# One channel tile of a 31-tap convolution: from VectorE's adds to products with diagonal matrices on TensorE

## The chip, the core and the metric

The kernel runs on one core of a Trainium2 chip. The metric is device time in microseconds (us). TensorE (PE in the rows) makes matrix products and writes them to PSUM, an on-chip memory of eight banks of 128 partitions by 512 fp32 values. VectorE (DVE), ScalarE (ACT) and GpSimd (POOL) work element by element; SyncE (SP) only issues DMA transfers here. Each engine executes its own instructions in the order of the program and waits where an operand isn't ready.

## What is computed

Two transformer blocks in fp32 on x of 512 tokens by 1024 channels. The first has a SwiGLU, two kinds of attention, gates and a second SwiGLU. The second has a mixer and a mixture of 32 experts. The change lies in the mixer:

```python
def hybrid_mixer(h, w_in, b_in, conv_w, conv_b, conv_ln_g, conv_ln_b, ...):
    z = jnp.einsum("bsd,de->bse", h, w_in) + b_in
    conv_a, conv_gate, q, k, v, o, i_pre, f_pre = jnp.split(z, ...)
    u = conv_a * jax.nn.sigmoid(conv_gate)
    u = causal_depthwise_conv(u, conv_w, conv_b)          # 31 taps, 512 channels
    u = jax.nn.silu(layernorm(u, conv_ln_g, conv_ln_b))
    qk = jax.nn.silu(causal_depthwise_conv(jnp.concatenate([q, k], axis=-1), qk_conv_w, qk_conv_b))
    ...                                                    # mlstm_chunkwise, 4 heads: hm
    y = jnp.concatenate([u, hm], axis=-1)
    return jnp.einsum("bse,ed->bsd", y, w_out)
```

A tap of the depthwise convolution multiplies a channel's row by one weight, shifts it by s tokens, and adds it to the sum.

## The kernel before

Activations lie with channels on the 128 partitions and the 512 tokens along the row, so 512 channels are four tiles. fp32 products are made of three fast ones: weights and activations are split into a high part and a rest (`hi` by a ScalarE copy, `lo` by a subtraction on VectorE or GpSimd), and high·high, high·rest and rest·high are added in a bank (`mm3`). `dense` is one output tile: 24 products for 1024 input channels. Its result lies in one of three banks with the tag `mm`, and VectorE must have read it before the bank is used again. Two banks have the tag `sc`, two `tp`, and one `po`.

`second_mixer` issues its work in this order:

- For each tile j of 0 to 3, two `dense` calls (the gate `cg` and `ca`). ScalarE makes the sigmoid, VectorE multiplies, and u_in[j] (named `ca` in rows) is ready.
- The recurrence gates: 24 products of the eight columns `wif`, read by VectorE as `zif`.
- `proj_rows`: 96 products for v into three `mm` banks and `po`. The gates' own chain (`recurrence`, tiles `ls_`, `ca_rows`, `cm_rows`, `em`) is issued between them, one step per point.
- Eight `dense` calls for q and k, each followed on VectorE by a 4-tap convolution (`late`, tiles `zq` and `qk`), and the four heads of the recurrence (`weights`, `head`; tiles `md`, `w`, `den`, `hm`).
- Four `dense` calls for the output gate `so`. Before the second, `conv_norm` issues what is left of the 31-tap convolution and starts its layer norm (`csum`, `csq`).
- The products with w_out, then the mixture of experts.

The 31-tap convolution writes `co[0]` to `co[3]` (`conv` in rows). VectorE makes tiles 0 and 1 and 19 taps of tile 2; ScalarE (multiply, `ctmp`) and GpSimd (add) make tile 3 and 12 taps of tile 2. GpSimd also makes the rests `wlo` of the weights. Where a tap stands is decided while the program is written: `fill` is called after and within the `dense` calls, and issues taps as long as VectorE's estimated work stays behind TensorE's by FILL[0]. The engines execute what this gives; nothing is decided on the chip.

Of the kernel before, what the change touches and what calls it, by code (L numbers as in the profile page):

```python
# [8 lines left out]
F32 = mybir.dt.float32  # L9
F32R = mybir.dt.float32r  # L10
I32 = mybir.dt.int32
BF16 = mybir.dt.bfloat16
AF = mybir.ActivationFunctionType
ALU = mybir.AluOpType
# [4 lines left out]
T = 512  # L19
# [49 lines left out]
    ("mlstm_norm_g_2", 4), ("subln_g", 1), ("conv_w", 124), ("qk_conv_w", 32),  # L69
]  # L70
VOFF = {}
_o = 0
# [62 lines left out]
def expert_stream(g, u, d):  # L135

    g = g.reshape(NE, 2, 4, 128, DE).transpose(0, 1, 3, 2, 4).reshape(NE, 2, 128, 2048)
    u = u.reshape(NE, 2, 4, 128, DE).transpose(0, 1, 3, 2, 4).reshape(NE, 2, 128, 2048)
    d = d.reshape(NE, 2, 2, 128, D).transpose(0, 1, 3, 2, 4).reshape(NE, 2, 128, 2048)
    return np.ascontiguousarray(np.stack([g[:, 0], u[:, 0], g[:, 1], u[:, 1], d[:, 0], d[:, 1]], axis=1))  # L140
# [13 lines left out]
def constants():  # L154
    c = np.zeros((128, 128 * 4 + 512 + 242), np.float32)
    i = np.arange(128)
    c[:, 0:128] = np.eye(128)
    c[:, 128:256] = 1.0
    c[:, 256:384] = i[:, None] < i[None, :]
    c[:, 384:512] = np.where(i[:, None] <= i[None, :], 0.0, BIG)  # L160
    c[:, 512:1024] = np.arange(512)[None, :]
    r = c[:, 1024:]
    r[:, 0] = i
    r[:, 1] = 128 * i
    r[:, 2:74] = np.arange(72)[None, :]
    r[:, 74:106] = NE - np.arange(NE)[None, :]
    r[:, 106:110] = 128 * np.arange(4)[None, :] + i[:, None] - 1024
    r[:, 110:114] = 128 * np.arange(4)[None, :]
    r[:, 114:242] = (i % 64)[None, :]
    rel = np.arange(640) - 511  # L170
    b = t5_bucket_of(rel)
    hot = np.zeros((32, 640), np.float32)
    hot[b, np.arange(640)] = 1.0
    sel = np.zeros((8, 512), np.float32)
    for h in range(4):
        sel[4 + h, h * 128:(h + 1) * 128] = 1.0
    return c, hot, sel


def lay_out(a):  # L180

    r = {}
    r["xT"] = np.ascontiguousarray(a["x"][0].reshape(4, 128, KC, 128).transpose(3, 0, 2, 1))
    r["wd"] = dense_stream(a)
    r["we"] = expert_stream(a["expert_w_gate_2"][0], a["expert_w_up_2"][0], a["expert_w_down_2"][0])
    v = dict(a)
    v["b_in"] = a["b_in_2"][0, :3072]
    v["conv_w"] = a["conv_w_2"][0]
    v["qk_conv_w"] = a["qk_conv_w_2"][0]
    cols = [np.ascontiguousarray(v[n]).reshape(-1, 128).T for n, k in VECS]  # L190
    r["vecs"] = np.ascontiguousarray(np.concatenate(cols, axis=1))
    r["rows"] = np.ascontiguousarray(np.concatenate([
        a["b_in_2"][0, 2048:2560], a["norm_ffn_g_2"][0], a["final_norm_g_2"],
        a["router_group_b_2"][0], a["router_expert_b_2"][0],
        a["lambda_q1"][0], a["lambda_k1"][0], a["lambda_q2"][0], a["lambda_k2"][0]])[None])
    r["w_if"] = np.ascontiguousarray(a["w_in_2"][0][:, 3072:3080].reshape(KC, 128, 8).transpose(1, 0, 2))
    r["b_if"] = np.ascontiguousarray(a["b_in_2"][0, 3072:3080].reshape(8, 1))
    wr = np.concatenate([a["router_group_w_2"][0], a["router_expert_w_2"][0]], axis=1)
    r["w_r"] = np.ascontiguousarray(wr.reshape(KC, 128, 36).transpose(1, 0, 2))
    r["rel_a"] = a["rel_bias_a"][0]  # L200
    r["t5"] = np.ascontiguousarray(a["t5_bias"].T)
    r["c_main"], r["c_hot"], r["c_sel"] = constants()
    return r
# [5 lines left out]
class Stream:  # L209
# [35 lines left out]
    def next(self, n=1):  # L245
        u, j = divmod(self.pos, 8)
        if j == 0:
            self.split_to(u + HL - 1)
            self.hl.pop(u - 1, None)
        self.pos += n  # L250
        hi, lo = self.hl[u]
        s = slice(j * 128, (j + n) * 128)
        return hi[:, s], lo[:, s]
# [63 lines left out]
class Kern:  # L317
# [594 lines left out]
    def second_mixer(self):  # L912
        nc, I = self.nc, self.I
# [4 lines left out]
        u_in = []  # L918
        conv_ready = [-1]
# [12 lines left out]
        V = nc.vector  # L932
# [15 lines left out]
        sel = self.u("sel")  # L948
        nc.gpsimd.dma_start(sel[0:8, :], I["c_sel"][:, 0:512])

        def tile_taps(j):
            V.tensor_scalar(co[j], u_in[j], cw(j, 30), self.vec("conv_b_2", j), op0=ALU.mult, op1=ALU.add)
            yield 1
            for s in range(1, 31 - (POOL_TAPS if j == 2 else 0)):
                V.scalar_tensor_tensor(co[j][:, s:], u_in[j][:, :T - s], cw(j, 30 - s), co[j][:, s:],
                                       op0=ALU.mult, op1=ALU.add)
                yield 1

        def dve_taps():
            g = {j: tile_taps(j) for j in range(3)}  # L960
            while g:
                for j in list(g):
                    if conv_ready[0] >= j:
                        if next(g[j], 0):
                            yield 1
                        else:
                            del g[j]
                if g and min(g) > conv_ready[0]:
                    yield 0
                if conv_ready[0] < 0:  # L970
                    yield 0
        dtaps = dve_taps()

        co = [self.v("conv") for _ in range(4)]
# [22 lines left out]
        ptaps = pool_taps()  # L997
# [7 lines left out]

        def fill(spare=0.0):

            while V.work + FILL[0] + spare < nc.tensor.work:
                if next(dtaps, 0) == 0:
                    break  # L1010
            while nc.gpsimd.work + FILL[1] < nc.tensor.work:
                if next(ptaps, 0) == 0:
                    break
            V.work = max(V.work, nc.tensor.work)
            nc.gpsimd.work = max(nc.gpsimd.work, nc.tensor.work - FILL[2])
# [15 lines left out]
        def point():  # L1031
            stages.point()
            fill()
# [12 lines left out]
        for j in range(4):  # L1046
# [6 lines left out]
            g, a = self.u("cg"), self.v("ca")  # L1053
# [8 lines left out]

        ps = self.mm()
        for c in range(KC):
            self.mm3(ps[0:8], (whl[0][:, c], whl[1][:, c]), n[c], c == 0, c == KC - 1)
        fill()
# [63 lines left out]
        v = self.proj_rows(rr, bias=bv, hook=point)  # L1132
# [75 lines left out]

        def conv_norm():

            for g in (dtaps, ptaps):
                for _ in g:
                    pass
            if POOL_TAPS:
                V.tensor_add(co[2], co[2], co2)
            stages.start(layer_norm())
# [40 lines left out]
        for i in range(8):  # L1257
            h, which = divmod(i, 2)
            j = 4 * which + h
            point()  # L1260
            ps = self.dense(n, half)
# [19 lines left out]
        for j in range(4):  # L1281
# [6 lines left out]
            ps = self.dense(n, half)  # L1288
            late = None
            o = self.u("so")  # L1290
# [5 lines left out]
        for m in range(KC):  # L1296
# [4 lines left out]
            ps = self.dense(y)  # L1301
# [3 lines left out]
        for m in range(KC):  # L1305
            ps = self.dense(hm, self.mixed_sums if m == KC - 1 else None)
            for f in range(2 if m == KC - 1 else 1):
                a = slice(2 * f, 2 * f + 2) if m == KC - 1 else slice(0, 4)
# [626 lines left out]
```

## Time and profile before

| | |
|---|---|
| median of 3 runs | 2005.67 us (2005.52 to 2008.32) |
| the profiled execution: its time | 2004.82 us |
| its span | 2003.0 us |
| TensorE busy | 1894.3 us, 95% |
| VectorE busy | 1087.9 us, 54% |
| ScalarE, GpSimd busy | 636.4 us, 381.8 us |
| mean granted TensorE clock | 0.978 of full speed |

The span runs from the first to the last instruction; 1.8 us of the execution lie outside it. Times within the span are counted from its start. A matmul's busy time includes its way through the array, and it overlaps the next, so TensorE can be called busy while it isn't at its peak rate. The mixer lies at 1113 to 1430 us, the experts behind it.

### The profile page before, as it was taken

The page shows a single profiled execution, that of the slowest core. Times are in us where ns is not written, and L with a number is a line of the kernel's source. Part 1 is how long each engine was busy: PE and PEld are TensorE (multiplying, and loading weights), DVE is VectorE, ACT ScalarE, POOL GpSimd, SP SyncE. Part 2 cuts the span into 40 slices and gives each one's busy share as a digit, 9 for nine tenths or more (in the row PEclk, how much of TensorE's full clock was granted, in tenths as well). Part 3 has the DMA queues.
Part 4 walks back from the last instruction along what each step waited for, and adds up shares of the span by engine and source line. Part 5 has one row for each costly group of instructions (what it writes and reads, how often), then busy time and mean ns, then how long its engine had stood idle before and what let it go on. Part 6 is the DMA issues. An engine that isn't in the chain of part 4 may idle for free.

```text
span 2003.0 us, 22137 instructions
## 1 busy us (share of the span) xinstructions
PE 1894.3 (95%) x8372; PEld 1299.0 (65%) x8372; DVE 1087.9 (54%) x1655; ACT 636.4 (32%) x1006; POOL 381.8 (19%) x293
## 2 busy tenths in 40 slices
PE   7999999999999999999999988779799999999995
PEld 5888888887777788888888766657543333333331
DVE  6443344423668565443444599988544444444445
ACT  4322233325555443331223333433232111111112
POOL 2000000106654351000001456643210000000001
PEclk9999999999999999999999998889999999999997
DMA  5234222322222122222222211111799999999991
GB/s 178 85 129 153 92 97 93 126 85 93 81 68 75 64 93 97 101 89 106 86 104 101 97 63 43 42 42 54 288 355 420 419 397 391 380 397 378 384 359 43
DMA packets 52440, 337.85 MB, mean 169 GB/s; under 512 B 5868, under 2 KB 8724, under 8 KB 13804
## 3 DMA queue, kind: packets, MB, share of 16 engines
q1 hardware_dynamic: 48396, 324.04, 42.2%
q0 software_dynamic: 3072, 9.24, 1.5%
q10 hardware_dynamic: 864, 3.15, 0.4%
q8 instruction: 67, 1.10, 0.2%
q14 instruction: 41, 0.34, 0.0%
HBM read 332.18 MB, written 8.16 MB: 170 GB/s over the span
## 4 chain that ended last, share of the span: by engine, by line
PE 81%; DVE 14%; issue 2%; ACT 1%; DMA 1%; POOL 1%; SPq 0%; POOLq 0%; ACTq 0%; DVEq 0%
PE mm L302 65%; PE sc L302 8%; PE tp L302 4%; DVE conv L302 4%; PE po L302 3%; DVE qk L302 2%; DVE score L302 1%; DVE x L302 1%; DVE att_s L302 1%; DVE rs_t L302 1%; DVE rs_y L302 0%; DMA x<-in_xT_dram 0%; DVE hm L302 0%; DMA raw<-in_wd_dram 0%; DVE rs_r L302 0%
## 5 line engine op out<-in xcount | busy, mean ns | idle before, releaser
L302 PE MATMUL mm<-nhi,whi 128*128 128x512 f32 x1120 | 446.8, 399 | 13.3 <-ACT whi L356 9.4
L302 PE MATMUL mm<-nlo,whi 128*128 128x512 f32 x1120 | 439.1, 392 | 1.6 <-DVE nlo L302 1.6
L302 PE MATMUL mm<-nhi,wlo 128*128 128x512 f32 x1120 | 438.5, 392 | 0.7 <-DVE wlo L302 0.7
L356 ACT ACTIVATE whi<-raw 128x1024 fp32r<-128x1024 f32 x220 | 231.2, 1053 | 306.8 <-PE mm L302 119.0
L302 DVE TENSOR_TENSOR wlo<-raw,whi 128x1024 fp32r<-128x1024 f32 x155 | 198.1, 1279 | 208.9 <-ACT whi L356 208.9
L302 PE MATMUL mm<-eraw,xb 128*64 128x512 f32 (+1 forms) x992 | 272.9, 602 | 0.0
L302 PEld LDWEIGHTS mm<-nhi,whi 128*128 128x128 f32 x1120 | 211.8, 189 | 62.7 <-ACT whi L356 9.4
L302 PEld LDWEIGHTS mm<-nlo,whi 128*128 128x128 f32 x1120 | 211.6, 189 | 47.1 <-DVE nlo L302 4.5
L302 PEld LDWEIGHTS mm<-nhi,wlo 128*128 128x128 f32 x1120 | 211.4, 189 | 46.5 <-DVE wlo L302 1.7
L302 POOL TENSOR_TENSOR wlo<-raw,whi 128x1024 fp32r<-128x1024 f32 x65 | 163.5, 2520 | 150.9 <-ACT whi L356 125.1
L302 PEld LDWEIGHTS mm<-eraw,xb 128*64 128x64 f32 (+1 forms) x992 | 81.9, 145 | 130.3 <-issue 120.5
L302 PE MATMUL sc<-eraw,hT 128*64 128x512 f32 (+1 forms) x512 | 140.1, 602 | 0.0
L302 PE MATMUL mm<-hhi,whi 128*128 128x512 f32 x352 | 136.9, 389 | 0.0
L302 PE MATMUL mm<-hlo,whi 128*128 128x512 f32 x352 | 136.9, 389 | 0.0
L302 PE MATMUL mm<-hhi,wlo 128*128 128x512 f32 x352 | 136.9, 389 | 0.0
L302 POOL TENSOR_TENSOR acc<-sq,sq 128x512 f32<-128x512 f32 x6 | 8.7, 1456 | 579.6 <-ACT sq L455 579.6
L302 DVE TENSOR_TENSOR x<-x,po 128x512 f32<-128x512 f32 x62 | 42.6, 687 | 125.4 <-PE po L302 125.3
L302 POOL TENSOR_SCALAR rs_v<-fss 128x1 f32<-128x1 f32 x3 | 0.6, 191 | 515.0 <-ACT eraw L1882 514.8
L1699 ACT ACTIVATE xb<-xs 128x512 f32 (+1 forms) x31 | 21.9, 706 | 233.1 <-PE mm L302 233.0
L302 DVE TENSOR_TENSOR up<-mm,row 128x512 f32<-128x512 f32 x44 | 30.4, 691 | 110.8 <-PE mm L302 110.8
L302 DVE SCALAR_TENSOR_TENSOR conv<-ca,vecs,conv 128x502 f32<-128x502 f32 (+18 forms) x78 | 88.0, 1183 | 0.2
L302 DVE TENSOR_TENSOR y<-sc,y 64x512 fp32r<-64x512 f32 (+1 forms) x64 | 44.1, 689 | 80.7 <-ACT y L1774 62.3
(448 smaller groups left out, 2641.7 us busy)
## 6 DMA issues: line engine op xcount, KB each, us to landing
eraw<-in_we_dram SPq DMA_DIRECT2D x192, 1024.0 KB, 8.0
raw<-in_wd_dram SPq DMA_DIRECT2D x109, 1024.0 KB, 4.8
bias_rows<-bias_by_distance SPq DMA_DIRECT2D x4, 960.0 KB
bias<-bias_rows POOLq DMA_DIRECT2D x12, 256.0 KB, 3.1
x_rows<-x ACTq DMA_DIRECT2D x4, 512.0 KB, 3.5
x<-in_xT_dram SPq DMA_DIRECT2D x3, 512.0 KB, 8.3
raw<-in_wd_dram SPq DMA_DIRECT2D x2, 512.0 KB, 8.9
out_dram<-eraw SPq DMA_DIRECT2D x2, 512.0 KB
```

The source lines that it names most:

```text
L302: return f(*a, **k)
L356: self.nc.scalar.activation(hi, raw, AF.Copy)
L1699: self.nc.scalar.activation(x[:, :, 0:m], self.xs[:, :, ds(row, m)], AF.Copy)
```

## The change

Tile 0 of the convolution leaves VectorE. A new generator, `pe_taps`, advances by one step at every `fill`. It splits tile 0's weights and u_in[0] into high part and rest. For each four taps ScalarE then makes eight diagonal matrices of 128x128 (identity times a weight column, `cdh` and `cdl`), and TensorE adds three products a tap into one bank of the `sc` ring, shifted by the tap. A shift must be even, so an odd tap starts one column later, and one VectorE operation on 15 columns adds what is left out. The weight table gets 31 more columns (`conv_r`). The gates' product takes the other `sc` bank in place of an `mm` bank.

```diff
+        def pe_taps():
+            while conv_ready[0] < 0:
+                yield 0
+            o = VOFF["conv_r"]
+            w = self.vecs[:, o:o + 31]
+            wd = self.u("cwd", F32R)
+            wd = wd[:, 0:31], wd[:, 31:62]
+            self.split_act(w, *wd)
+            uh, ul = self.u("cuh", F32R), self.u("cul", F32R)
+            self.split_act(u_in[0], uh, ul)
+            p = self.sc()
+            yield 1
+            for s0 in range(0, 31, 4):
+                m = range(s0, min(s0 + 4, 31))
+                d = self.u("cdh", F32R), self.u("cdl", F32R)
+                for t, a in zip(d, wd):
+                    for i, s in enumerate(m):
+                        nc.scalar.activation(t[:, i * 128:(i + 1) * 128], self.ident, AF.Copy,
+                                             scale=a[:, s:s + 1].bitcast(F32))
+                yield 1
+                for i, s in enumerate(m):
+                    dh, dl = (t[:, i * 128:(i + 1) * 128] for t in d)
+                    for a, b in ((dh, uh), (dh, ul), (dl, uh)):
+                        nc.tensor.matmul(p[:, s + s % 2:], a, b[:, s % 2:T - s], start=(s == 0 and a is dh and b is uh),
+                                         stop=(s == 30 and a is dl))
+                yield 1
+            nc.scalar.activation(co[0], p, AF.Identity, bias=self.vec("conv_b_2", 0))
+            V.scalar_tensor_tensor(co[0][:, 1:30:2], w[:, 1:30:2], u_in[0][:, 0:1], co[0][:, 1:30:2],
+                                   op0=ALU.mult, op1=ALU.add)
...
-            g = {j: tile_taps(j) for j in range(3)}
+            g = {j: tile_taps(j) for j in (1, 2)}
...
         def fill(spare=0.0):
+            next(petaps, 0)
...
-        ps = self.mm()
+        ps = self.sc()
         for c in range(KC):
             self.mm3(ps[0:8], (whl[0][:, c], whl[1][:, c]), n[c], c == 0, c == KC - 1)
...
-            for g in (dtaps, ptaps):
+            for g in (petaps, dtaps, ptaps):
```

The taps that stay on VectorE move forward. Before, in its instructions behind `zif` (the gates' product, just ahead of v), taps of the tiles conv_8100 (0), conv_8101 (1) and conv_8102 (2) stand between the steps of the recurrence, and go on up to `conv_norm`:

```order
L302 TENSOR_TENSOR zif_8500<-mm_8454,RR_8231 8x512
L302 COPY zt_8531<-tp_8526 128x32
L302 SCALAR_TENSOR_TENSOR conv_8101<-ca_8294,vecs,conv_8101 128x501
L302 SCALAR_TENSOR_TENSOR conv_8102<-ca_8371,vecs,conv_8102 128x506
L302 TENSOR_SCALAR ls_s_8534<-ls_e_8533 128x16
```

In the changed program, in the same place, the last tap of all stands ahead of `zif`, and behind it comes nothing of the convolution but the 15 columns:

```order
L303 SCALAR_TENSOR_TENSOR conv_8102<-ca_8460,vecs,conv_8102 128x495
L303 SCALAR_TENSOR_TENSOR conv_8102<-ca_8460,vecs,conv_8102 128x494
L303 TENSOR_TENSOR zif_8686<-sc_8621,RR_8231 8x512
L303 COPY zt_8717<-tp_8712 128x32
L303 TENSOR_SCALAR ls_s_8720<-ls_e_8719 128x16
```

So 50 operations for tiles 1 and 2 stand ahead of `zif` in place of 32 for tiles 0 to 2, none ahead of u_in[1], and the q and k stretch has none.

On ScalarE the diagonals stand between the sigmoids (`cg`) and the weights' high parts (`whi`); `ctmp` are the first products of GpSimd's taps. This is the changed program around the fourth tile's sigmoid (`cg_8605`), where before there was nothing between it and `conv`:

```order
L357 ACTIVATE whi_8543<-raw_8395 128x1024
L970 ACTIVATE cdh_8559<-cmain,cwd_8258 128x128 x4
L970 ACTIVATE cdl_8560<-cmain,cwd_8258 128x128 x4
L1090 ACTIVATE cg_8605<-cg_8605,vecs 128x512
L970 ACTIVATE cdh_8611<-cmain,cwd_8258 128x128 x4
L970 ACTIVATE cdl_8612<-cmain,cwd_8258 128x128 x4
L1016 ACTIVATE conv_8103<-ca_8606,vecs 128x512
L1019 ACTIVATE ctmp_8665<-ca_8606,vecs 128x511
```

The group that `cdh_8611` feeds stands behind a sigmoid that waits for VectorE.

On TensorE that group stands between the gates' product (`sc_8621`) and the first product of v (`mm_8692`), which followed each other before:

```order
L303 MATMUL sc_8621<-nhi_8063,wif_1352_8079 8x512
L303 MATMUL sc_8621<-nlo_8064,wif_1352_8079 8x512
L303 MATMUL sc_8621<-nhi_8063,wif_1353_8080 8x512
L303 MATMUL sc_8265<-cuh_8261,cdh_8611 128x488
L303 MATMUL sc_8265<-cul_8262,cdh_8611 128x488
L303 MATMUL sc_8265<-cuh_8261,cdl_8612 128x488
...
L303 MATMUL mm_8692<-whi_8397,nhi_7719 128x512
```

Six groups of 12 products stand ahead of the gates' product, this one behind it, and the last (9 products) behind the second of the eight steps of v. It waits for diagonals that ScalarE makes behind `zif` and the first two `ls_e`.

## Rows read from the trace of the kernel before

**Rows 1.** The page: VectorE's and TensorE's busy tenths in 40 slices (50 us each), granted clock.

```profile
PE   7999999999999999999999988779799999999995
DVE  6443344423668565443444599988544444444445
PEclk9999999999999999999999998889999999999997
```

**Rows 2.** The chain that ended last, by line, of 1147 to 1229 and 1229 to 1344.

```profile
by line: DVE conv L302 45.8%; PE mm L302 23.1%; issue 9.9%; PE po L302 7.1%; PE tp L302 4.9%; DVE ca L302 3.7%; ACT cg L1055 3.6%; DVE cg L302 2.3%; DVE zif L302 0.7%; DVE em L302 0.0%
by line: DVE qk L302 38.4%; DVE conv L302 32.9%; issue 5.1%; DVE csum L302 4.5%; ACT zq L1274 4.5%; DVE zq L302 4.2%; DVE w L302 4.2%; DVE vr L302 2.3%; DVE md L302 2.0%; DVE den L302 1.1%; ACT so L1292 0.6%; DVE hm L302 0.6%; DVE so L302 0
```

**Rows 3.** Windows: stretch, length, busy us (instructions) of each engine, granted clock, DMA.

```profile
core 0: us, PE busy (x) PEld busy (x) DVE busy (x) ACT busy (x) POOL busy (x), PEclk, DMA share, GB/s
1147.00:1192.00 45.00, 38.99 (x168) 29.27 (x166) 41.57 (x45) 14.32 (x18) 17.24 (x8) 0.96 0.14 47
1192.00:1229.00 37.00, 28.43 (x108) 22.01 (x108) 30.87 (x47) 14.96 (x22) 26.56 (x15) 0.79 0.16 58
1229.00:1344.00 115.00, 88.96 (x400) 68.74 (x400) 106.76 (x120) 44.21 (x82) 70.62 (x43) 0.88 0.13 46
```

**Rows 4.** Waits of TensorE at 1185 to 1344: in total, times, longest.

```profile
PE tp L302 <- DVE den L302: 18.3, 3, 9.1
PE tp L302 <- issue: 6.0, 1, 6.0
PE mm L302 <- DVE zif L302: 5.5, 1, 5.5
PE mm L302 <- DVE vr L302: 3.9, 1, 3.9
```

**Rows 5.** Windows of the tile conv alone (VectorE's, ScalarE's, GpSimd's part of the convolution).

```profile
1158.00:1184.00 26.00, 23.02 (x23) 0.00 (x0) 0.00 (x0) 1.00 0.24 81
1192.00:1224.00 32.00, 13.56 (x19) 0.00 (x0) 14.59 (x10) 0.76 0.19 67
1224.00:1239.00 15.00, 12.12 (x7) 0.00 (x0) 8.26 (x6) 0.89 0.19 70
```

**Rows 6.** Timeline of VectorE and GpSimd at 1158 to 1230: start, us, operation.

```profile
1158.00 0.75 DVE L302 SCALAR_TENSOR_TENSOR ca<-ca,vecs,cg 128x512 f32<-128x512 f32 x1 [0.20 <-ACT cg L1055]
1158.79 0.55 DVE L302 TENSOR_SCALAR conv<-ca,vecs 128x512 f32<-128x512 f32 x1
1191.60 0.67 DVE L302 TENSOR_TENSOR zif<-mm,RR 8x512 f32<-8x512 f32 x1
1208.66 2.68 DVE L302 SCALAR_TENSOR_TENSOR conv<-ca,vecs,conv 128x497 f32<-128x497 f32 x4
1218.40 6.49 POOL L302 TENSOR_TENSOR conv<-conv,ctmp 128x501 f32<-128x501 f32 x2
1220.48 3.29 DVE L302 SCALAR_TENSOR_TENSOR conv<-ca,vecs,conv 128x502 f32<-128x502 f32 x5
1223.93 5.89 DVE L302 SCALAR_TENSOR_TENSOR conv<-ca,vecs,conv 128x495 f32<-128x495 f32 x3
1224.85 2.81 POOL L302 TENSOR_TENSOR wlo<-raw,whi 128x1024 fp32r<-128x1024 f32 x1
```

**Rows 7.** The chain in order of time: an undisturbed run of products.

```profile
695.05 76.18 PE mm L302 x336
```

**Rows 8.** Timeline of ScalarE: three 128x128 operations in a row.

```profile
1247.68 0.39 ACT L1151 ACTIVATE w<-md,ca 128x128 f32<-128x128 f32 x1
1247.98 0.39 ACT L1153 ACTIVATE w<-mb,ca 128x128 f32<-128x128 f32 x1
1248.27 0.39 ACT L1151 ACTIVATE w<-md,ca 128x128 f32<-128x128 f32 x1
```

**Rows 9.** Timeline of TensorE: the end of `wif`, starts of v, of q, and of the norm.

```profile
1183.97 0.39 PE L302 MATMUL mm<-nhi,wif 128*8 128x512 f32 x1
1192.33 0.79 PE L302 MATMUL mm<-whi,nhi 128*128 128x512 f32 x1 [5.53 <-DVE zif L302]
1230.63 0.47 PE L302 MATMUL mm<-nhi,whi 128*128 128x512 f32 x1 [3.86 <-DVE vr L302]
1344.30 2.07 PE L302 MATMUL tp<-csum,cmain 128*128 128x512 f32 x2 [2.85 <-DVE csum L302]
```

**Rows 10.** Groups of VectorE at 1229 to 1344: busy, mean ns.

```profile
L302 DVE SCALAR_TENSOR_TENSOR conv<-ca,vecs,conv 128x491 f32<-128x491 f32 (+17 forms) x29 | 38.3, 1364 | 0.1
L302 DVE SCALAR_TENSOR_TENSOR qk<-zq,vecs,qk 128x511 f32<-128x511 f32 (+2 forms) x24 | 30.2, 1258 | 0.8
```

**Rows 11.** Groups of GpSimd at 1186 to 1344.

```profile
L302 POOL TENSOR_TENSOR conv<-conv,ctmp 128x492 f32<-128x492 f32 (+29 forms) x41 | 60.3, 1470 | 30.7 <-ACT ctmp L985 26.5 <-ACT ctmp L994 2.0
L302 POOL TENSOR_TENSOR wlo<-raw,whi 128x1024 fp32r<-128x1024 f32 x14 | 36.3, 2596 | 15.3 <-ACT whi L356 15.3
L302 POOL TENSOR_TENSOR hm<-hm,row 128x512 f32<-128x512 f32 x3 | 5.0, 1675 | 18.0 <-ACT row L430 18.0
```

**Rows 12.** Windows behind the mixer: the experts' stretch, columns as in the third group.

```profile
1450.00:1600.00 150.00, 146.44 (x628) 57.85 (x630) 72.33 (x138) 35.78 (x76) 7.53 (x9) 0.98 0.98 396
1600.00:1750.00 150.00, 150.00 (x560) 55.59 (x556) 69.05 (x110) 27.06 (x45) 0.00 (x0) 1.00 0.98 391
```

More of the change, by code (lines that the diff above doesn't have):

```diff
@@ L68 @@
     ("conv_b_2", 4), ("conv_ln_g_2", 4), ("conv_ln_b_2", 4), ("qk_conv_b_2", 8),
-    ("mlstm_norm_g_2", 4), ("subln_g", 1), ("conv_w", 124), ("qk_conv_w", 32),
+    ("mlstm_norm_g_2", 4), ("subln_g", 1), ("conv_w", 124), ("qk_conv_w", 32), ("conv_r", 31),
 ]
@@ L189, in lay_out @@
     v["qk_conv_w"] = a["qk_conv_w_2"][0]
+    v["conv_r"] = a["conv_w_2"][0][::-1, 0:128]
     cols = [np.ascontiguousarray(v[n]).reshape(-1, 128).T for n, k in VECS]
@@ L949, in second_mixer @@
         nc.gpsimd.dma_start(sel[0:8, :], I["c_sel"][:, 0:512])
+        def pe_taps():
[27 more added lines that the diff above has]
+                                   op0=ALU.mult, op1=ALU.add)
+        petaps = pe_taps()
         def tile_taps(j):
```

## Prediction

> **What bounds the kernel now.** The first view is the page's table of slices [rows 1]. TensorE is at 9 tenths nearly everywhere, except in a dip in slices 24 to 29 (8 8 7 7 9 7), where VectorE is at its fullest (9 9 9 8 8 from slice 24). There lies the second mixer. The second view, the chain of work that ended last, read for the mixer alone [rows 2], shows why: at 1147 to 1229 us VectorE's taps (`conv`) hold 45.8% of it, TensorE's `mm` 23.1%; at 1229 to 1344 VectorE's `qk` holds 38.4%, its taps 32.9%, and TensorE is hardly there. The third, the windows [rows 3], gives the room: at 1229 to 1344 VectorE is busy 106.76 us of 115, TensorE 88.96, at a granted clock of 0.88; at 1192 to 1229 TensorE is busy 28.43 of 37. The fourth, TensorE's waits [rows 4], names VectorE each time: for `den` 18.3 us, `zif` 5.5, `vr` 3.9, and 6.0 put down to nothing while the recurrence's small VectorE steps run between taps. So in this stage, and only here, a tap on VectorE is on the path, and work on TensorE partly isn't.
>
> Ahead of 1184 it is the other way. TensorE runs the first dense products and `wif` without a gap, the last of them at 1183.97 [rows 9], while VectorE lags behind. Work put in there is paid in full.
>
> **What the change removes.** 31 operations (one on tensor and scalar, 30 two-tensor adds) leave VectorE. Two prices stand in the rows. In the mean a tap took 1.36 us at 1229 to 1344 [rows 10] and 1.00 at 1158 to 1184 (23.02 by 23) [rows 5]. But four taps in a row took 2.68, or 0.67 each, while GpSimd was idle [rows 6]. What lies between is GpSimd: five taps took 3.29 while two GpSimd adds took 6.49, against 1.47 for one in the mean [rows 6, 11]; and three taps took 5.89 around a `wlo` of 2.81 [rows 6]. One side stands while the other runs. If a tap's blocked time goes away with it, 31 taps at (1.00+1.36)/2 = 1.18 give 36.6 us. If the blocked time goes to the next operation, they give 31 x 0.67 = 20.8.
>
> The Trainium skill, "SBUF — State Buffer", section "Who interferes with whom", says that VectorE and GpSimd share one pair of ports as an exclusive lock: a VectorE instruction with two SBUF inputs and a GpSimd instruction that reads SBUF wait for each other, for the whole instruction. By that rule GpSimd's hold on the port stays and a tap gives back its own 0.67, so the stage could gain 20.8 us at most; by the mean price 36.6. The trace agrees with it in both directions in the rows just read. I take the sum below, which counts stretch by stretch, and keep 36.6 for the low end.
>
> **What it adds.** TensorE: 93 products of 496.5 columns in the mean (512 less the even shifts 0 to 30). 336 products of 512 columns took 76.18 us, 0.227 each [rows 7], so 0.22 each and 20.5 us in all. ScalarE: 62 diagonals. Operations of this size start 0.30 us apart [rows 8], so 18.6 us, two thirds of them ahead of 1192, where ScalarE is busy 14.32 of 45 [rows 3]: room enough, except where a group stands behind something late (below). VectorE: two subtractions and the 15 columns, together below 1.5 us, the first two while it would wait for u_in[1]: nothing. The wider weight table is 31 columns more in a load of 269: nothing. The bank of the `sc` ring is read by ScalarE during v, before a head asks for it: nothing; without that cover head 0 would wait for the rest of v.
>
> **The stage, stretch by stretch.**
>
> First, up to v. VectorE has nothing to do for tile 0 now and starts its taps when u_in[1] is there, at about 1158 as before [rows 6]. 50 operations stand ahead of `zif` in place of 32; before it came at 1191.6. At 0.67 to 1.00 they take 34 to 50 us; with 4 us for the two later tiles' gates `zif` comes at 1196 to 1212. I take 1206, nearer the end that this stretch showed. TensorE: 1184 plus seven groups of 12 at 0.22 = 18.5 gives 1202.5; the seventh waits for diagonals made behind the fourth sigmoid, which stands six taps ahead of `zif`, so at about 1200 plus 3 us. v starts at about 1206 in place of 1192.3 [rows 9]: 14 us later.
>
> Second, v until the first product of q. Before it took 38.3 us (1192.3 to 1230.6 [rows 9]), of which 6.0 and 3.9 are waits [rows 4] and the clock stood at 0.79 [rows 3]. Now 96 products at 0.227 are 21.8, the last 9 diagonal ones 2.0, the recurrence's small products about 2, a wait for the last diagonals (behind `zif` and a table load on ScalarE) 2 to 4, and the read of the first bank 1.5: 31 us. VectorE has no taps between the recurrence's steps, so the 6.0 shrinks. q starts at 1237 in place of 1230.6: +6.5. Bounds: +1 (taps at 0.67 and no wait) to +15 (taps at 1.00, both waits in full).
>
> Third, q and k until the norm's first product, 113.7 us before (1230.6 to 1344.3 [rows 9]). VectorE loses its 29 taps, 38.3 us [rows 10], and is left with 106.76 - 38.3 = 68.5. So TensorE's 88.96 is now the larger. It holds some overlap and half-clock time; all of it at full clock would be 0.88 x 88.96 = 78. On the other side some waits for `den` stay. I take 88, that is -25.7, with bounds 80 and 100: -34 to -14.
>
> Behind that nothing is removed. The experts' stretch is full of transfers (DMA share 0.98 [rows 12]) and starts when the mixer ends, so what the mixer gives is kept.
>
> Sum: +6.5 - 25.7 = -19.2, bounds -33 to +1. The profiled execution's 2004.82 becomes 1985.6. That execution lies 0.85 below the median of 2005.67, so about **1986 us**. 0.2%, or 4 us, is about what a measurement of this kernel can tell from no change.
>
> **The rivals.**
>
> *A tap is worth its mean price.* TensorE's front is no longer lengthened by VectorE, and q and k fall to 80: -33 to -36, 1970. For it: the taps' 1.36 in the mean [rows 10]. Against: the pairs of rows in which one engine stands while the other works [rows 6].
>
> *GpSimd is last.* Its part of the convolution can start only with u_in[3], now at about 1201, and it needs 60.3 + 36.3 + 5.0 = 101.6 us for taps, rests and heads [rows 11], so until 1303 without a pause. It paused 30.7 + 15.3 + 18.0 = 64 us, mostly for ScalarE. By the forecast the norm comes at 1325, so more than 22 us of pauses decide it; with half of them it ends at 1335, and the time is 1996. Against: those pauses came from ScalarE waiting for VectorE's `qk`, which comes earlier now.
>
> *Slower: the taps jam the front.* At 1224 to 1239, with GpSimd's adds running, a tap took 1.73 us (12.12 by 7 [rows 5]). 50 at that price are 86 us in place of the 44 taken: v starts 42 us later still, and the kernel takes about 2028. It decides from a tap of 1.27 us in the front. Against: GpSimd has only `wlo` to make there until u_in[3], and the 23 operations at 1158 to 1184 had exactly that beside them.
>
> *No gain.* The waits for `den` come from the q and k convolutions and not from the taps; the third stretch stays at 107 and pays only for the front: 2005.
>
> **How the numbers follow.** The forecast (gain of 14 to 27, 1979 to 1992) 0.55, the mean price 0.14, GpSimd last 0.16, no gain 0.07, slower 0.08. So faster 0.85, same 0.07, slower 0.08. The likeliest one's own range is 1979 to 1992. For 8 in 10 the range takes in GpSimd's case up to 2001 and the mean price down to 1973, and leaves out the slower case, nearly all of the even one, and the far end of the mean price.
>
> **What the profile of the changed kernel would show.** Step by step: products `sc` from `cuh` and `cul` about 0.22 us apart; `zif` on VectorE at about 1206 and the first product of v just ahead of or behind it; a wait of TensorE on ScalarE's `cdh` or `cdl` of a few us in all, not at each of the eight groups; q from about 1237; no `conv` on VectorE behind `zif` but the 15 columns; VectorE well below full in q and k, TensorE near full there, waits for `den` well below 18.3; `csum` at about 1325; everything behind it 19 us earlier, with the same lengths. The forecast would be wrong if TensorE waits for diagonals group by group (dense products late), if taps in the front cost over 1.2, or if `csum` waits for GpSimd.

## The result

The changed kernel takes **2018.93 us** (median of 4 runs, 2016.75 to 2026.01) against 2005.6 (2004.72 to 2008.32) before. The ratio is 1.007, 95% interval [1.0056, 1.0083], so it is slower. Forecast was 1986 us, with a range up to 2001.

The profiled execution of the changed kernel takes 2017.67 us, with a span of 2015.8. The page of it, VectorE, TensorE and the granted clock in 40 slices, answers to [rows 1]:

```profile
PE   7999999999999999999999998989799999999995
DVE  6443344433557665443344487798545444444455
PEclk9999999999999999999999998999999999999997
```

The dip of the second mixer is there as before and has become shallower (slices 24 to 29: 9 8 9 8 9 7 in place of 8 8 7 7 9 7). That fits a gain, and no slice shows where time was lost. The loss shows when one asks at what time the mixer begins. VectorE's first gate in it, before (first fence) and after (second):

```profile
1148.10 0.69 DVE L302 TENSOR_TENSOR cg<-mm,RR 128x512 f32<-128x512 f32 x1 [2.03 <-ACT RR L430]
```

```profile
1171.75 0.69 DVE L303 TENSOR_TENSOR cg<-mm,RR 128x512 f32<-128x512 f32 x1 [2.03 <-ACT RR L431]
```

It comes 23.65 us later. Of what the change adds only the wider load of the weight table lies ahead of it. So the time is lost in code that the diff doesn't touch. What fills that part is TensorE's dense products, and the chain of after, in order of time, has the same undisturbed run of 336 of them as [rows 7]:

```profile
707.79 78.08 PE mm L303 x336
```

78.08 us in place of 76.18: 0.2324 us a product in place of 0.2267, at a full granted clock in both. Ahead of the mixer stand 4525 such products; 0.0057 us on each would be 25.8 us.

Inside the mixer the change did gain. TensorE's timeline of after, the rows that answer to [rows 9]:

```profile
1224.50 0.39 PE L303 MATMUL sc<-nhi,wif 128*8 128x512 f32 x1
...
1228.82 0.39 PE L303 MATMUL mm<-whi,nhi 128*128 128x512 f32 x1
...
1267.95 0.39 PE L303 MATMUL mm<-nhi,whi 128*128 128x512 f32 x1
...
1358.43 1.12 PE L303 MATMUL tp<-csum,cmain 128*128 128x512 f32 x2 [2.85 <-DVE csum L303]
```

From the first gate to the norm's product it is 1358.43 - 1171.75 = 186.7 us, before 1344.30 - 1148.10 = 196.2: 9.5 us gained of the 19.2 forecast. The windows of after cut the mixer at the rows above (columns as in [rows 3]):

```profile
1171.00:1216.00 45.00, 45.00 (x194) 36.72 (x193) 37.74 (x44) 24.32 (x61) 13.11 (x5) 0.98 0.15 53
1216.00:1229.00 13.00, 12.10 (x52) 7.04 (x52) 12.63 (x20) 4.73 (x12) 0.27 (x1) 1.00 0.01 1
1229.00:1268.00 39.00, 30.18 (x124) 23.76 (x124) 22.97 (x32) 18.84 (x33) 30.96 (x22) 0.87 0.15 55
1268.00:1358.40 90.40, 83.58 (x401) 64.22 (x399) 76.13 (x90) 44.48 (x81) 62.65 (x38) 0.98 0.16 59
```

TensorE has no gap in the first, which now holds the gates' product and most of the diagonal ones. In the last it is busy 83.6 of 90.4 us, where it was 88.96 of 115. In between lies v's stage, 39 us long and only 30 of it busy. TensorE's waits from 1209 to 1358, which answer to [rows 4], say where:

```profile
PE tp L303 <- issue: 7.1, 1, 7.1
PE tp L303 <- DVE den L303: 3.3, 2, 3.0
PE tp L303 <- ACT zif L1106: 1.7, 1, 1.7
```

The waits for `den` are nearly gone (3.3 us, 18.3 before), those of v's products for VectorE's `zif` and `vr` are gone, and the one put down to nothing has grown from 6.0 to 7.1. It ends at the product of `ls_f`, which needs the recurrence's small VectorE steps. The timeline of VectorE and GpSimd there:

```profile
1238.07 2.33 DVE L303 TENSOR_TENSOR ls_q<-ls_s 128x16 f32<-128x16 f32 x1
1240.44 1.21 DVE L303 TENSOR_SCALAR ls_p<-ls_q 128x16 f32<-128x16 f32 x1
1241.69 6.01 DVE L303 SCALAR_TENSOR_TENSOR ls_p<-ls_p,ls_q 128x16 f32<-128x16 f32 x7
1247.73 1.16 DVE L303 SCALAR_TENSOR_TENSOR ls_p<-ls_p,ls_s 128x16 f32<-128x16 f32 x1
...
1237.96 2.41 POOL L303 TENSOR_TENSOR wlo<-raw,whi 128x1024 fp32r<-128x1024 f32 x1
1240.33 5.03 POOL L303 TENSOR_TENSOR conv<-conv,ctmp 128x504 f32<-128x504 f32 x4
1245.32 2.34 POOL L303 TENSOR_TENSOR wlo<-raw,whi 128x1024 fp32r<-128x1024 f32 x1
1247.62 2.55 POOL L303 TENSOR_TENSOR conv<-conv,ctmp 128x500 f32<-128x500 f32 x2
```

Operations on 16 columns take 1.16 to 2.33 us, about as long as the GpSimd operation beside each. Behind the mixer nothing has changed: 657.4 us to the end of the span, 658.7 before.

So two things are to be explained: 23.65 us lost ahead of the mixer, and half of the gain in it.

### The profile page after: what moved, and what is told of

It reads as the page before. It is cut to its first block, busy times and chain, and to the rows that moved or that the text cites. A ratio compares the mean times of both kernels' runs of the same rounds, so it can differ in the third digit from the quotient of the medians.

```text
span 2015.8 us, 22365 instructions
## 1 busy us (share of the span) xinstructions
PE 1936.0 (96%) x8465; PEld 1313.7 (65%) x8465; DVE 1055.8 (52%) x1627; ACT 655.8 (33%) x1071; POOL 375.2 (19%) x293
## 4 chain that ended last, share of the span: by engine, by line
PE 83%; DVE 11%; ACT 2%; issue 2%; DMA 1%; POOL 1%; SPq 0%; POOLq 0%; DVEq 0%; ACTq 0%
PE mm L303 68%; PE sc L303 8%; PE tp L303 4%; PE po L303 3%; DVE qk L303 2%; DVE conv L303 2%; DVE x L303 1%; DVE rs_t L303 1%; DVE score L303 0%; DMA x<-in_xT_dram 0%; DVE hm L303 0%; DVE rs_y L303 0%; ACT ctmp L1019 0%; DVE att_s L303 0%; DMA raw<-in_wd_dram 0%
## 5 line engine op out<-in xcount | busy, mean ns | idle before, releaser
L303 PE MATMUL mm<-nhi,whi 128*128 128x512 f32 x1120 | 451.8, 403 | 9.0 <-ACT whi L357 9.0
L303 PE MATMUL mm<-nlo,whi 128*128 128x512 f32 x1120 | 444.6, 397 | 0.5 <-DVE nlo L303 0.5
L303 PE MATMUL mm<-nhi,wlo 128*128 128x512 f32 x1120 | 444.1, 397 | 0.7 <-DVE wlo L303 0.7
L303 PEld LDWEIGHTS sc<-eraw,hT 128*64 128x64 f32 (+1 forms) x512 | 41.6, 144 | 66.3 <-issue 61.5
```

Source lines behind the costliest of these rows:

```text
L303: return f(*a, **k)
```

## The experiments

All of these kernels do the whole computation. "a_" kernels are the changed kernel with an edit, "b_" kernels the kernel before with one.

### Where the tiles stand

**Theory A**: the 31 columns in the weight table, which is allocated early, move every tile that is allocated behind it on the left side of the memory 128 bytes up (124 bytes, rounded to 32-byte steps), and the products' time depends on where their operands stand. **Rivals**: B, the added instructions slow TensorE's stream; C, the mixer's new work costs the time.

`b_pad128` is the kernel before with an unused tile behind the table:

```
         self.vecs = self.cpool.tile([128, NV], F32, name="vecs")
+        self.cpool.tile([128, 32], F32, name="pad")
```

`b_pad256`, `b_pad64` and `b_pad32` have 64, 16 and 8 columns in place of 32. `a_tri` is the changed kernel with the reversed taps in free columns of the mask's tile, so that nothing moves:

```
-    ("mlstm_norm_g_2", 4), ... ("conv_w", 124), ("qk_conv_w", 32), ("conv_r", 31),
+    ("mlstm_norm_g_2", 4), ... ("conv_w", 124), ("qk_conv_w", 32),
...
         nc.gpsimd.dma_start(tri[:, 0:256], I["c_main"][:, 256:512])
+        nc.gpsimd.dma_start(tri[:, 256:287], I["conv_r"])
...
-            w = self.vecs[:, o:o + 31]
+            w = tri[:, 256:287]
```

> The kernel before, with 128 bytes per partition left unused behind the weight table, so that every tile allocated after it (the landed weights, the split weights, the residual, the left-hand work tiles) stands 128 bytes higher, where the change also put them; not one instruction is added. Theory A, place: the 512-column products are slowed by where their operands stand. Then they take 0.2325 us instead of 0.2267 here too, the first normalization of the mixer's channels comes some 24 us later, and the whole kernel takes about 2030 us. Theory B, program: the added instructions or their place in the instruction stream slow TensorE. Then nothing moves: 0.2267 us and 2005 us. Theory C, the mixer's own new work alone costs the time: 2005 us as well.

> The changed kernel, but the reversed taps of tile 0 are loaded into 31 unused columns of the tile that holds the triangular mask, instead of into 31 more columns of the weight table: all tiles stand where they stood before, and the mixer's work is that of the change. One small load on GpSimd's queue is added. Theory A, place: products at 0.2267 us again, the mixer begins at 1148 us as before, and the kernel gains what the mixer alone gains, 9.5 us by the two traces: about 1996 us. Theory B, program: products still at 0.2325 us, about 2018 us. Theory C, the mixer's own work: 2018 us with the products at 0.2267 us.

> The kernel before with 256 unused bytes behind the weight table instead of 128, no instruction added. Theory A in the form that a period of 256 bytes matters: as before, 0.2267 us a product and 2005 us. In the form that any move against the operands on the other side of the memory matters: 0.23 us or more and 2020 to 2035 us. Theory B: 2005 us.

> The kernel before with 32 unused bytes behind the weight table, no instruction added. Theory A in the form that 64 bytes matter: slower products, 2015 to 2035 us, or faster ones than 0.2267 us if the place before was itself not the best (0.2157 us would give about 1960 us). In the form that only 128 bytes matter: 2005 us. Theory B: 2005 us.

`b_pad128` took 2028.76 us, ratio 1.0112 [1.0095, 1.0129], without an instruction added. `a_tri`, with all the work of the change, took 1996.62 us, ratio 0.9958 [0.9942, 0.9975]. The same 336 products in the chain of `b_pad128` (first fence) and `a_tri` (second):

```profile
709.74 78.08 PE mm L302 x336
```

```profile
694.70 76.18 PE mm L303 x336
```

These are the two values of after and before to the last digit. B and C fall, A stands: the place costs 2028.76 - 2005.44 = 23.3 us on the kernel before and 2018.93 - 1996.62 = 22.3 us on the changed one.

Next was whether the weights' own address counts (A2) or how far they stand from the moving tiles (A1). The split weights lie on the left, the normalized channels and hidden halves on the right, in a pool that fills the memory from its other end. An unused tile in that pool moves them down:

```
                 self.first()
+                self.u2.tile([128, 32], F32, name="rpad", tag="rpad", bufs=1)
```

> The kernel before; nothing on the left is moved, but 128 bytes per partition are left unused on the right side, so that the normalized channels and the hidden halves (the moving operands of the dense products) stand 128 bytes lower. No instruction added. Theory A1, the distance: what counts is how the split weights on the left stand to the moving tiles on the right, modulo 256 bytes. Then the products take 0.232 to 0.234 us and the kernel 2025 to 2032 us, as with 128 bytes on the left. Theory A2, the weights' own address: 0.2267 us and 2005 us, since no weight moves.

> The kernel before with 128 unused bytes on both sides: the split weights 128 bytes higher, the moving tiles 128 bytes lower, so both stand at another address, and 256 bytes closer to each other. No instruction added. Theory A1, the distance modulo 256 bytes: 0.2267 us a product and 2005 us. Theory A2, the weights' own address (or either one's own): 0.2325 us and 2025 to 2032 us.

> The kernel before with the weights 32 bytes higher and the moving tiles 224 bytes lower: the distance between them shrinks by 256 bytes, and both now start at a multiple of 256 bytes. No instruction added. Theory A1 (only the distance counts): 0.2267 us and 2005 us. If the start itself counts as well, products below 0.2267 us: at 0.2133 us for 512 columns at the granted 2.4 GHz (worked out as 512 columns by one each clock) the some 4700 products would give about 60 us back, 1945 us.

> The kernel before with 64 unused bytes behind the weight table, no instruction added. Theory A1 with a period of 256 bytes and every other distance slow: 0.232 to 0.234 us and 2025 to 2032 us. With a period of 64 bytes it would be 2005 us, but 128 bytes were slow, so this is not expected.

The times of before and `b_pad128` are medians of four runs, the others single runs; the kernel before took 2008.29 us beside `b_right128`, `b_both128`, `b_both_0` and `b_pad64`. The table gives for each kernel how far the distance between weights and moving tiles shrinks, and what the run of 336 products took in its chain:

| kernel | left up, right down, bytes | distance shrinks by | 336 products, us | time, us |
|---|---|---|---|---|
| before | 0, 0 | 0 | 76.18 | 2005.6 |
| b_pad32 | 32, 0 | 32 | 78.39 | 2029.89 |
| b_pad64 | 64, 0 | 64 | 78.41 | 2035.39 |
| b_pad128 | 128, 0 | 128 | 78.08 | 2028.76 |
| b_right128 | 0, 128 | 128 | 78.39 | 2028.53 |
| b_both128 | 128, 128 | 256 | 76.21 | 2004.67 |
| b_both_0 | 32, 224 | 256 | 76.21 | 2007.4 |
| b_pad256 | 256, 0 | 256 | 76.18 | 2005.97 |

Theory A1, that the distance counts, fits every row of products. With the weights unmoved (`b_right128`) the products slow down, and with both moved but the distance changed by 256 (`b_both128`, `b_both_0`) they don't. In the built programs the distance is a multiple of 256 bytes in the table's four kernels where the 336 products take 76.2 us (before, the split weights start at byte 57056 of a partition and the moving tiles at 147424, 353 times 256 apart) and in none of the other four. The hope that a start at a multiple of 256 bytes is better still (`b_both_0`) was a miss. `b_pad64` lies 3 us above its range and 5.5 above `b_pad32`, whose products cost the same; why isn't shown, and both are single runs. A control lies inside the traces: the 96 products of `hmhi` and `hmlo` have both operands on the left, so that a pad moves both or neither. Where one follows another without a pause, their starts are 229.6 ns apart in the mean before, 229.8 after and 230.2 in `b_pad128`, so they don't follow the pads.

### Where the other half of the gain went

With the tiles in place the mixer of `a_tri` can be held against that of before without the shift: the first gate at 1147.51, v at 1205.11, q at 1244.31, the norm's product at 1334.71. Its windows of v's stage and of q and k:

```profile
1205.00:1244.00 39.00, 30.13 (x124) 23.89 (x123) 22.84 (x33) 19.11 (x33) 30.71 (x21) 0.87 0.15 55
1244.00:1334.70 90.70, 82.79 (x403) 64.51 (x401) 76.56 (x90) 44.47 (x81) 63.04 (x39) 0.98 0.17 58
```

v's stage was forecast at 31 us. **Theory P**: GpSimd's adds stretch the recurrence's steps. **Rival T**: TensorE's diagonal products and half-clock time there. All kernels from here on are `a_tri` with a further edit. `a_hold` keeps GpSimd's part of the convolution back until the recurrence has its sums:

```
-            while nc.gpsimd.work + FILL[1] < nc.tensor.work:
+            while not hold[0] and nc.gpsimd.work + FILL[1] < nc.tensor.work:
...
-            nc.gpsimd.work = max(nc.gpsimd.work, nc.tensor.work - FILL[2])
+            nc.gpsimd.work = max(nc.gpsimd.work, nc.tensor.work - (6.0 if hold[0] else FILL[2]))
...
             conv_ready[0] = j
+            hold[0] = j == 3
...
             nc.vector.tensor_sub(ca[:, :, 4:8], zi, ca[:, :, 0:4])
             yield
+            hold[0] = False
```

`a_late` starts the convolution on TensorE only behind the gates' product, three steps at each point; `a_hold_late` has both edits:

```
+            for _ in range(pe_steps[0]):
-            next(petaps, 0)
+                next(petaps, 0)
...
+        pe_steps[0] = 3
         fill()
         zif = self.u("zif")
```

> Against the changed kernel with its tiles back in their old places (a_tri, 1996.6 us): GpSimd's part of the convolution is held back from the fourth gate until the recurrence has its sums, so that no GpSimd add runs beside the recurrence's small steps; nine adds move behind them. Theory P, GpSimd's adds: the steps on 16 columns took 0.8 to 1.2 us each because they alternate with adds of 1.25 us on a shared port; without adds the chain from the first to the last of them shrinks from 16.5 to about 6 us, TensorE's wait of 7.1 us disappears, q starts 7 to 9 us earlier (1236 in place of 1244.3), and the time is 1987 to 1990 us. Theory T, TensorE's own work: the diagonal products left in that stage and the lower clock behind waits make the stage 39 us long; then nothing moves, 1995 to 1998 us. Rival L: the adds are missing at the end, the norm waits for GpSimd, and the time is 1996 to 2006 us with a short recurrence.

> Against a_tri (1996.6 us): the convolution on TensorE begins only behind the gates' product, three steps at each point, so that all 93 diagonal products lie between the products of v instead of between the dense products ahead of it. If the products are paid in full wherever they stand, the gates' product ends 18 us earlier (1182 to 1184), v begins at 1190 to 1193, its stage lasts 55 us or more, and the time stays at 1995 to 1999 us. If they fit into the waits for zif (7 us) and for the recurrence (7.1 us), q starts at 1232 to 1238 in place of 1244.3 and the time is 1984 to 1990 us. If ScalarE cannot make 62 diagonals (18.6 us) beside the splits of the weights there, TensorE waits for cdh and cdl: over 2000 us.

> Both edits together, against a_tri (1996.6 us). If GpSimd's adds stretch the recurrence and the waits there are the room into which the products fit, the two compete for the same room: 1983 to 1990 us, no better than the better of the two by more than 3 us. If they are independent, their gains add.

`a_hold` took 1991.39 us, ratio 0.993 [0.9913, 0.9946]. VectorE and GpSimd in the recurrence of `a_hold`, the steps of the fence on after:

```profile
1211.83 0.17 DVE L303 TENSOR_TENSOR ls_q<-ls_s 128x16 f32<-128x16 f32 x1
1212.04 0.17 DVE L303 TENSOR_SCALAR ls_p<-ls_q 128x16 f32<-128x16 f32 x1
1212.25 3.59 DVE L303 SCALAR_TENSOR_TENSOR ls_p<-ls_p,ls_q 128x16 f32<-128x16 f32 x7
1215.88 0.17 DVE L303 SCALAR_TENSOR_TENSOR ls_p<-ls_p,ls_s 128x16 f32<-128x16 f32 x1
...
1208.87 2.40 POOL L303 TENSOR_TENSOR wlo<-raw,whi 128x1024 fp32r<-128x1024 f32 x1 [21.30 <-ACT whi L357]
1213.21 2.39 POOL L303 TENSOR_TENSOR wlo<-raw,whi 128x1024 fp32r<-128x1024 f32 x1 [1.94 <-ACT whi L357]
```

0.17 us in place of 1.16 to 2.33. Of these only the seven steps that the second `wlo` falls into still take 3.59 us, which is 2.39 and seven times 0.17. From the copy of the transposed gates to the last sum the recurrence takes 8.6 us (1208.35 to 1216.95) in place of 16.8, and v's stage 27 us with TensorE busy throughout. Windows of `a_hold`, v's stage and q and k:

```profile
1205.00:1232.00 27.00, 26.73 (x124) 21.06 (x124) 13.45 (x32) 15.69 (x27) 14.93 (x9) 1.00 0.23 79
1232.00:1330.50 98.50, 86.03 (x402) 66.51 (x400) 84.28 (x90) 49.26 (x89) 79.77 (x51) 0.93 0.15 54
```

TensorE does the same 124 products in both, so T falls. The edit also holds back ScalarE's first products (`ctmp`) that feed the adds, but they are not what stretched the steps: in `a_hold` none runs beside the seven steps, and in `a_tri` ScalarE stands idle from 1219.2 on while the steps stay long until 1225. Rival L did not come either: GpSimd's last add ends at 1317.3, `csum` starts at 1325.2. Still the time lies 1.4 us above the range that P gave, though q starts 4 us earlier than P said: of the 12.2 us gained in v's stage 8.0 are lost in the next (98.44 from q's first product to the norm's, in place of 90.40). The adds that were held back run there, and VectorE's work on q and k gets dearer by as much. Windows of the tile `qk` alone (columns as in [rows 3]; VectorE's third) between those two products, of before, `a_tri` and `a_hold`:

```profile
1230.60:1344.30 113.70, 13.02 (x32) 7.07 (x32) 47.65 (x48) 5.05 (x8) 0.00 (x0) 0.88 0.13 47
1244.30:1334.70 90.40, 10.94 (x32) 5.78 (x32) 55.16 (x48) 5.04 (x8) 0.00 (x0) 0.98 0.17 59
1232.00:1330.50 98.50, 13.75 (x32) 7.14 (x32) 63.10 (x48) 5.04 (x8) 0.00 (x0) 0.93 0.15 54
```

The dearest groups of VectorE and GpSimd, of `a_tri` at 1232 to 1335 (first fence) and of `a_hold` at the same times (second):

```profile
L303 DVE SCALAR_TENSOR_TENSOR qk<-zq,vecs,qk 128x511 f32<-128x511 f32 (+2 forms) x24 | 30.9, 1289 | 0.8
L303 POOL TENSOR_TENSOR conv<-conv,ctmp 128x492 f32<-128x492 f32 (+16 forms) x28 | 38.4, 1372 | 13.6 <-ACT ctmp L1019 12.1
```

```profile
L303 DVE SCALAR_TENSOR_TENSOR qk<-zq,vecs,qk 128x511 f32<-128x511 f32 (+2 forms) x24 | 36.7, 1528 | 0.9
L303 POOL TENSOR_TENSOR conv<-conv,ctmp 128x492 f32<-128x492 f32 (+24 forms) x36 | 48.4, 1345 | 12.3 <-ACT ctmp L1019 10.3
```

The first fence opens 12 us before `a_tri`'s first product of q: between the two products 35 adds start in `a_hold` and 23 in `a_tri`. Twelve adds more, and the same 24 operations take 36.7 us in place of 30.9, all 48 on `qk` 63.1 in place of 55.2.

`a_late` took 1999.99 us (0.9967 [0.9955, 0.9978]) and `a_hold_late` 1999.76 (0.9971 [0.9961, 0.9981]), 3 us worse than `a_tri`. In `a_late` v starts at 1192.7, 12.4 us earlier than in `a_tri`, but its stage lasts 61.3 us and q starts 9.7 us later than in `a_tri`. TensorE's waits at 1147 to 1350 of `a_late`:

```profile
PE tp L303 <- DVE ca L303: 7.9, 1, 7.9
PE sc L303 <- ACT cdh L970: 5.1, 2, 2.7
```

The products don't fit into the recurrence's waits. They are paid in full (TensorE is busy 47.7 us of v's stage in place of 30.1), the diagonals come late as well (`cdh`, 5.1 us), and the recurrence, with VectorE's taps between its steps, stays long (`ca`, 7.9 us). With the adds held back the late products still cost 8.4 us against `a_hold`, and holding the adds back gains nothing once the products are late: neither of the two cases expected for `a_hold_late` came.

The last pair asks whether GpSimd's adds are paid by VectorE wherever they run. Twelve taps of tile 2 go back from ScalarE and GpSimd to VectorE:

```
-POOL_TAPS = 12
+POOL_TAPS = 0
```

> Against a_hold (1991.4 us): twelve taps of tile 2 that ScalarE and GpSimd made go back to VectorE (the constant for them is 0 in place of 12), so GpSimd makes 11 adds and one fill less, some 14 to 16 us of its work, and VectorE makes 12 taps and no final add more. Theory P, every GpSimd add is paid by whatever VectorE does beside it: the q and k operations on VectorE shrink from 1.53 towards 1.0 us each (24 of them, 36.7 us), which gives back 10 to 14 us against 12 taps of 0.67 (8 us); the stretch from q to the norm's product falls from 98.4 to 90 to 95 us and the time to 1984 to 1989 us. Theory V, VectorE is simply the busiest engine there: 8 us more work on it make it 2 to 8 us longer, 1993 to 2000 us.

> The same constant in a_tri (1996.6 us), where GpSimd's adds still run beside the recurrence. Theory P: v's stage stays at 39 us, the stretch behind it falls from 90.4 to 85 to 88 us: 1991 to 1995 us. Theory V: it grows to 92 to 98 us, 1998 to 2004 us.

`a_tri_p0` took 1992.19 us (0.9936 [0.992, 0.9953]), `a_hold_p0` 1989.74 (0.9921 [0.9905, 0.9938]), the fastest here. Groups of `a_tri_p0` at 1244 to 1332 (first fence) and of `a_hold_p0` at 1232 to 1330 (second):

```profile
L303 DVE SCALAR_TENSOR_TENSOR qk<-zq,vecs,qk 128x511 f32<-128x511 f32 (+2 forms) x24 | 27.7, 1155 | 0.8
L303 POOL TENSOR_TENSOR conv<-conv,ctmp 128x495 f32<-128x495 f32 (+13 forms) x14 | 18.5, 1321 | 12.8 <-ACT ctmp L1019 12.1
```

```profile
L303 DVE SCALAR_TENSOR_TENSOR qk<-zq,vecs,qk 128x511 f32<-128x511 f32 (+2 forms) x24 | 33.3, 1386 | 0.8
L303 POOL TENSOR_TENSOR conv<-conv,ctmp 128x509 f32<-128x509 f32 (+27 forms) x28 | 37.3, 1334 | 12.7 <-ACT ctmp L1019 11.1
```

Twelve operations more on VectorE, and the stretch from q to the norm gets shorter in both: 84.9 us in place of 90.4, and 92.7 in place of 98.4. VectorE's 48 operations on `qk` show why, of `a_tri_p0` and `a_hold_p0`:

```profile
1247.50:1332.40 84.90, 9.40 (x32) 5.14 (x32) 50.40 (x48) 5.04 (x8) 0.00 (x0) 1.00 0.17 62
1237.90:1330.70 92.80, 11.20 (x32) 6.14 (x32) 58.16 (x48) 5.03 (x8) 0.00 (x0) 0.96 0.16 57
```

They give back 4.8 and 4.9 us, with 11 and 12 adds fewer in the stretch. So P holds there. The stretch isn't a test of V, since none of the twelve taps stands in it. They are paid ahead of q: q starts at 1247.5 in place of 1244.3, and at 1237.9 in place of 1232.0. In the sum V has the wrong sign, but little is left over. For `a_hold_p0` the gain is smaller than P said (1989.7, expected 1984 to 1989), and against `a_hold`, on another chip, its 1.7 us are within the intervals; the 4.4 us of `a_tri_p0` against `a_tri` are a difference of medians whose intervals still touch. The edit takes twelve products from ScalarE as well. Its `ctmp` holds 3.4% of the chain from q to the norm in `a_tri` and 1.5% in `a_tri_p0`, 1.8 us less, so a part of the 5.5 us gained there can be ScalarE's; no run separates the two.

## Why the prediction was wrong

**The step that decided it** is "The wider weight table is 31 columns more in a load of 269: nothing." The load itself costs nothing that shows: `b_pad128` has none and loses as much. But the table is a tile, what is allocated behind it moves up by 128 bytes, and with that the dense products ahead of the mixer get dearer, in the undisturbed run 0.2324 us in place of 0.2267 [rows 7]: 22.3 us in the whole time (`a_tri` against the changed kernel). None of the rivals had it: all of them, the slower one too, lay inside the mixer. Without it the result is that of `a_tri`, 1996.6, faster and inside the range.

**v at 1206**: right in the number, partly by luck. 1205.1 in `a_tri`, 57.6 us behind the first gate; in the changed kernel 57.1 behind it. The forecast took 1206 from `zif`, which came at 1208.24, and v did not wait for it: TensorE's own products, which the forecast had ending by about 1203, ended at 1205.1 and decided. The window of VectorE's part of the convolution ahead of it in `a_tri` (VectorE, ScalarE, GpSimd busy):

```profile
1147.00:1208.20 61.20, 44.73 (x50) 0.80 (x1) 3.03 (x3) 0.98 0.10 35
```

The 50 operations took 44.73 us, 0.89 each, where 44 were taken; so the rival of taps at 1.27 us did not come. TensorE waited for `cdh` and `cdl` 1.1 and 0.5 us in all. One thing in it was misread: the row at 1192.33 in [rows 9] is not v's first product. Six stand ahead of it, before the wait for the bank that `zif` frees:

```profile
1185.17 0.47 PE L302 MATMUL mm<-whi,nhi 128*128 128x512 f32 x1 [0.81 <-DVE cg L302]
```

So v's first product moved by 19.9 us. That is 18.5 for the 84 added products that stand ahead of it, at the forecast's price, and 1.6 of waits for their diagonals. The wait of 5.5 us behind the first six is gone; the gates' product now lies in a bank of the scores' ring. Counted from 1192.33, as the forecast did, the move is 12.8 of its 14 us.

**v's stage, 31 us**: wrong, 39.2. The step that failed is "VectorE has no taps between the recurrence's steps, so the 6.0 shrinks." There were no taps, and it grew to 7.1: GpSimd's adds took their place beside the steps. They now start at 1205 with the fourth gate and run through the whole recurrence; before, GpSimd had run out of them from 1207 to 1216. `a_hold` shows it: without adds there, 27 us, below the forecast. The sum of 31 had no term for this wait and none for the clock behind the waits: 15 of v's products in `a_tri` start 0.43 us apart, at the lower of the clock's two levels (0.87 granted over the stage), about 3 us more than at 0.23; in `a_hold`, without the waits, the granted clock is 1.00. Q came 13.7 us later than before, not 6.5.

**q and k, 88 us**: close, 90.4, so -23.3 in place of -25.7. The picture behind the number was half right. In `a_tri` TensorE is busy 82.8 of 90.7 us and the waits for `den` fell to 3.9, as forecast; but in the changed kernel VectorE's `qk` still holds 48.0% of the chain there. The step that was off is "VectorE loses its 29 taps, 38.3 us [rows 10], and is left with 106.76 - 38.3 = 68.5." It is left with 76.6, mostly because its 48 operations on `qk` took 7.5 us more when the taps were gone (47.65 and 55.16 above). A part of the taps' blocked time went to the next operations, the case that the forecast had named, but this step priced the taps at their mean. What stretches `qk` is GpSimd, as the adds of `a_hold` and of the last pair measured. That 88 came so close is in part luck.

*GpSimd is last* did not come: its last add ends at 1307.1 in `a_tri`, and `csum` starts at 1329.4, with 1325 forecast.

**The sum for the mixer**: +13.7 - 23.3 = -9.6 us, against +6.5 - 25.7. `a_tri` measures 2005.44 - 1996.62 = 8.8. Of the 10.4 missing, 6.9 could be had back: by holding the adds (5.2 us against `a_tri`), by giving taps back to VectorE (4.4), with both 6.9. These are medians of different chips, on which the kernel before agrees within 0.6 us.

The Trainium skill, "SBUF — State Buffer", section "Who interferes with whom", has the rule that the forecast weighed: a VectorE instruction with two inputs in SBUF and a GpSimd instruction that reads there exclude each other for the whole instruction. The trace agrees, and more sharply than the forecast used it: 16 columns cost 0.17 us alone and 1.16 beside an add. The same section gives TensorE two independent read ports, for the moving operand and for the weights, and says that TensorE never waits on anyone. No run here shows TensorE waiting on another engine's access; what the runs show is that the place of its operands has a price, 23.3 us in `b_pad128`.

**What stays open**: what in the memory makes the distance count. The runs show that it does, for these products, and that a distance 256 bytes shorter is like the old one; they don't show which access waits, nor whether the multiple of 256 is the whole rule, since only five distances were tried.

## What to carry to other kernels

A table that grows by a few columns is also a move of everything behind it: hold the built addresses of the hot operands against those of the old kernel, and when code that the diff doesn't touch gets slower by the same share everywhere, undo the move (put the new data into free columns) before judging the change. Work that leaves VectorE doesn't shorten what is left on it as long as GpSimd's two-input operations run beside it; give GpSimd's adds a place where VectorE has nothing urgent, short dependent steps least of all.

## What was not expected of the hardware

- A 512-column fp32r product took 0.2267 us when the distance between its weights' tile and its moving tile was that of before or 256 bytes less, and 0.2324 to 0.2334 when it was 32, 64 or 128 less, at the same granted clock (1.00 in the stretch of the 336): 2.5 to 2.9% on the product, 1.0 to 1.4% on the kernel. Other distances were not tried.
- Where the products take longer they are also uneven: starts in `b_pad128` and after lie 228 to 241 ns apart, where before they are 226 or 227 for hundreds of products.
- A subtraction on 3 columns of q and k took 1.30 us in the mean (8 of them, 10.4 us, in `a_tri`), as long as a GpSimd add.
